# Slots of each expert place from one-hot products on the chip, in place of a slot table in device memory

## The chip, the cores and the metric

The kernel runs on one core of a Trainium2 chip. The metric is the device time of one execution in microseconds (us). Three runs of the kernel before took 1507.99 us in the median (1507.69 to 1508.86).

## The reference

One layer of a hybrid encoder over 512 tokens of width 1024: attention heads of three kinds, a layer norm, then a mixture of 32 experts, of which each token uses four, and a second layer norm. Only the routing and the experts matter here:

```python
def moe_ffn(x2d, router_w, router_b, w_gu, b_gu, w_dn, b_dn):
    logits = (x2d @ router_w + router_b).astype(jnp.float32)
    top_val, top_idx = lax.top_k(logits, TOP_K)          # TOP_K = 4 of 32
    gates = jax.nn.softmax(top_val, axis=-1)
    ...                                                  # rows sorted by expert
    def expert_block(args):
        xb, e = args
        hh = xb @ w_gu[e] + b_gu[e]
        glu = jnp.minimum(hh[:, 0::2], SWIGLU_LIMIT)
        lin = jnp.clip(hh[:, 1::2], -SWIGLU_LIMIT, SWIGLU_LIMIT)
        act = glu * jax.nn.sigmoid(SWIGLU_ALPHA * glu) * (lin + 1.0)
        return act @ w_dn[e] + b_dn[e]
    ...
    out = jnp.zeros((T, D), jnp.float32).at[row_tok].add(ys * row_gate[:, None])
```

An expert's weights are 8 MB for `w_gu` and 4 MB for `w_dn`, all in float32, so the 32 experts read some 400 MB from device memory.

## The kernel before

**Front part.** Projections, attention heads and the output projection (`w_o`) run for about 345 us. The 512 tokens are handled as four tiles of 128 (`tt` = 0 to 3). For each tile the residual row is normed (`normed`, ACT, DVE and POOL share it), written to `h_dram` by a POOL DMA, routed (`best_four`), given its position within each expert (`positions`) and its gate weights (`gates`).

**Places.** The experts are worked through in 32 places. Experts 0 and 1 have places 0 and 1, so their weights can be loaded before routing is known; the rest are ranked by how many tokens they have (`ranks`: `rank`, then `place`, a one-hot matrix from place to expert, and `eid`, the expert of each place). `TILES` says how many groups of 32 tokens a place has: three for most, two for the small ones (odd places 3 to 25, 30 and 31), four for place 12. Tokens beyond that go through a spare loop (`For_i`, L1220) whose count `ntrip` (computed in `rounds`) is read at run time; it has no trip in the profiled execution. At the entry of that loop SP waits on the semaphores of all DMA queues and the engines wait for one another.

**Slots.** A place must know for each of its slots the token to gather, the row of `y_dram` that its result is scattered to, and the gate. Before, this comes from a table in device memory. `table_rows` (DVE) works out the row of the table for each token and choice; `table_write` (POOL) writes four indirect DMAs per token tile, 16 in all. During place 0 `table_read` reads the table back with 13 DMAs issued by ACT into `TT`, in four variants of how slots lie on partitions, and `table_fit` adjusts them. `slots_of(e)` then picks one place's column out of `TT` with a multiplication, a sum and a cast on DVE. Place 1 alone, whose rows are needed early, gets its tokens from `slot_map` and `slots` (a float32 one-hot product).

**Loop over the places.** For place `e`, PE runs eight steps `k` of `gu_cols` (`hh`, L1088), then four of `dn_cols` of place `e-1` (`yy`, L1101). In between, in an order written out by hand for all engines (`manual_schedule`), stand the transposes of the activations (`thalf_cols`, L1147), the bias product (`bias_rows`, L1110) and the transposes of the next place's gathered rows (`transposed_rows`, L1074). These short products share two PSUM buffers `pt`; `hh` has one buffer only, so that place `e+1` cannot begin before DVE has read place `e`. `prepare(e+2)` at step `k` = 4 computes the slots of place `e+2` and gathers its rows; `store` scatters the results (L1166).

**Weights.** SP loads them in pieces of 1 MB, twelve per place, into a ring of 18 buffers (`raw`, `refill`, L896 and L898). Eighteen pieces are issued before place 0 starts; every further one waits until PE has finished with a buffer. From place 2 on the address comes from `eidI`.

Of the kernel before, what the change touches and what calls it, by code (L numbers as in the profile page):

```python
# [9 lines left out]
F32 = mybir.dt.float32  # L10
# [12 lines left out]
E, TOPK = 32, 4  # L23
# [14 lines left out]
def tile_encoder_layer(ctx: ExitStack, tc: tile.TileContext, a, out, dbg=None, stage=9):  # L38
# [622 lines left out]
    itok = lx.tile([P, 2, NT], F32, name="itok")  # L661
# [12 lines left out]
    posm = cst.tile([P, NT, E], F32, name="posm")  # L674
    R = cst.tile([P, NT, E, 3], F32, name="R")
# [60 lines left out]
    def positions(tt):  # L736

        dense = rt_w[tt][1]
        p = bank([P, E])
        for u in range(tt):  # L740
            nc.tensor.matmul(p, ones, sel[:, u, :], start=(u == 0), stop=False)
        nc.tensor.matmul(p, before, sel[:, tt, :], start=(tt == 0), stop=True)
        nc.vector.scalar_tensor_tensor(posm[:, tt, :], p, 1.0, dense, op0=OP.add, op1=OP.mult)
        nc.vector.tensor_scalar(posm[:, tt, :], posm[:, tt, :], -1.0, None, op0=OP.add)

    def gates(tt):
# [4 lines left out]
        over_k(R[:, tt, :, 2], eq[:, 1])  # L751
        nc.vector.tensor_mul(eq[:, 1], eq[:, 0], ik.unsqueeze(2).to_broadcast(b3))
        over_k(R[:, tt, :, 1], eq[:, 1])
        nc.vector.tensor_scalar(R[:, tt, :, 1], R[:, tt, :, 1], itok[:, 1, tt:tt + 1], None, op0=OP.add)
        nc.vector.tensor_copy(R[:, tt, :, 0], itok[:, 0, tt:tt + 1].to_broadcast([P, E]))

    def table_rows(tt):

        eq, _, g4, _ = rt_w[tt]
        nc.vector.tensor_copy(pay[:, tt, :, 2], g4)  # L760
        sx = lx.tile([P, E + TOPK], F32, name="sx", tag="sx", bufs=2)
        nc.vector.scalar_tensor_tensor(sx[:, 0:E], posm[:, tt, :], float(E), ie, op0=OP.mult, op1=OP.add)
        nc.vector.tensor_mul(eq[:, 1], eq[:, 0], sx[:, 0:E].unsqueeze(1).to_broadcast(b3))
        nc.vector.tensor_reduce(sx[:, E:E + TOPK], eq[:, 1], axis=AX.X, op=OP.add)
        nc.vector.tensor_copy(tix[:, tt, :], sx[:, E:E + TOPK])

    def table_write(tt):
        for k in range(TOPK):
            nc.gpsimd.indirect_dma_start(
                out=table[:, :], out_offset=bass.IndirectOffsetOnAxis(ap=tix[:, tt, k:k + 1], axis=0),  # L770
                in_=pay[:, tt, k, :], in_offset=None, bounds_check=P * E - 1, oob_is_err=False)
# [7 lines left out]
    def ranks(p):  # L779

        key, rank, eid = (mb.tile([P, E], F32, name=n) for n in ("key", "rank", "eid"))
# [5 lines left out]
        nc.vector.tensor_reduce(rank, w, axis=AX.X, op=OP.add)  # L787
        place = mb.tile([P, E, E], BF16, name="place")
# [6 lines left out]
        return rank, eid, eidI, place  # L795
# [26 lines left out]
    def places(tt):  # L822
# [3 lines left out]
        nc.vector.tensor_tensor(o, islot, posm[:, tt, 0:1].to_broadcast([P, P]), op=OP.is_equal)  # L826
# [27 lines left out]

    rp = mb.tile([P, E], F32, name="rp")
# [12 lines left out]
    pay = mb.tile([P, NT, TOPK, 3], F32, name="pay")  # L868
    nc.gpsimd.iota(pay[:, :, :, 0], pattern=[[P, NT], [0, TOPK]], base=0, channel_multiplier=1,
                   allow_small_or_imprecise_dtypes=True)  # L870
    nc.gpsimd.iota(pay[:, :, :, 1], pattern=[[TOPK * P, NT], [1, TOPK]], base=0, channel_multiplier=TOPK,
                   allow_small_or_imprecise_dtypes=True)
    table = dram.tile([P * E, 3], F32, name="table")
    empty = lx.tile([P, E, 3], F32, name="empty")
    nc.gpsimd.memset(empty[:, :, 0:2], float(BIG))
    nc.gpsimd.memset(empty[:, :, 2:3], 0.0)
    nc.gpsimd.dma_start(raw_ap(table, 0, [[3 * E, P], [1, 3 * E]]), empty.rearrange("p e c -> p (e c)"))
    tix = mb.tile([P, NT, TOPK], I32, name="tix")
# [107 lines left out]
    table_rows(0)  # L986
    table_write(0)
    places(0)
    table_rows(1)
# [12 lines left out]
    table_write(1)  # L1002
# [6 lines left out]
    table_rows(2)  # L1009
# [3 lines left out]
    table_write(2)  # L1013
# [11 lines left out]
    table_rows(3)  # L1025
# [15 lines left out]
    rank, eid, eidI, place = ranks(p)  # L1041
# [128 lines left out]
    def store(p, s, n):  # L1170
        y = mz.tile([P, 2, 512], F32, name="y", tag="y", bufs=2)
        ix, g = s
        for t in range(1, n):
            b, o, c = t // 2, (0, 0, 0, 256)[t], (0, 512, 256, 256)[t]
            nc.scalar.activation(y[:, b, o:o + c], p[:, b, o:o + c], AF.Copy, scale=g[:, t, 2:3])  # L1175
            scatter(y[:, b, o:o + c], ix[:, t, 1:2], D // c)
# [7 lines left out]

    TT = mb.tile([P, 4, E, 3], F32, name="TT")

    def table_read():
        def rd(dst, v, slot0):  # L1190
            n = dst.stop - dst.start
            nc.scalar.dma_start(TT[dst, v].rearrange("p e c -> p (e c)"),
                                raw_ap(table, slot0 * 3 * E, [[3 * E, n], [1, 3 * E]]))

        rd(slice(0, P), 0, 0)
        for g in range(4):
            for v in range(1, 4):
                rd(slice(32 * g, 32 * g + 32), v, 32 * (g // 2 if v == 1 else v))

    def table_fit():  # L1200
        for v in range(1, 4):
            nc.vector.tensor_scalar(TT[:, v, :, 1], TT[:, v, :, 1], 2.0 if v == 1 else 4.0,
                                    half if v == 1 else quarter, op0=OP.mult, op1=OP.add)

    def slots_of(e):

        n = 4 if TILES[e] == 4 else 3 if TILES[e] == 3 else 2
# [12 lines left out]
    with tc.For_i(0, n, 1):  # L1220
# [79 lines left out]
        scatter(y, iy)  # L1300


    yl, sl, bias = [], {}, {}
    py, ph, glu, sg, lin, aT, xg = {}, {}, {}, {}, {}, {}, {}

    def prepare(e):
# [284 lines left out]
```

## Time and profile before

| | us |
|---|---|
| median of three timed runs | 1507.99 |
| the profiled execution, its own time | 1503.06 |
| its span in the trace | 1501.3 |
| PE busy in the span | 1363.9 (91%) |
| DVE busy | 480.4 (32%) |
| ACT busy | 299.5 (20%) |
| POOL busy | 144.1 (10%) |

The 16 DMA engines moved 469.66 MB, 313 GB/s over the span and around 400 GB/s in the last two thirds. PE's busy time counts pipelined products whose ends are modelled, so it doesn't say alone that PE is the limit. The trace's times count from the start of the span.

### The profile page before, as it was taken

The page shows a single profiled execution, that of the slowest core. Times are in us where ns is not written, and L with a number is a line of the kernel's source. Part 1 is how long each engine was busy: PE and PEld are TensorE (multiplying, and loading weights), DVE is VectorE, ACT ScalarE, POOL GpSimd, SP SyncE. Part 2 cuts the span into 40 slices and gives each one's busy share as a digit, 9 for nine tenths or more (in the row PEclk, how much of TensorE's full clock was granted, in tenths as well). Part 3 has the DMA queues.
Part 4 walks back from the last instruction along what each step waited for, and adds up shares of the span by engine and source line. Part 5 has one row for each costly group of instructions (what it writes and reads, how often), then busy time and mean ns, then how long its engine had stood idle before and what let it go on. Part 6 is the DMA issues. An engine that isn't in the chain of part 4 may idle for free. (4 is left out here: it accounts for less than half of the span.)

```text
span 1501.3 us, 27744 instructions
## 1 busy us (share of the span) xinstructions
PE 1363.9 (91%) x11708; PEld 622.4 (41%) x11708; DVE 480.4 (32%) x1137; ACT 299.5 (20%) x553; POOL 144.1 (10%) x174
## 2 busy tenths in 40 slices
PE   7999998993449989999999989999998989999995
PEld 6888786893113323332332323332232322333232
DVE  5697658674321111211121111211111121111138
ACT  4345557410011111111111111111111111111110
POOL 3000000022310010001000011010100000000013
PEclk9999998897679999999999999999999999999888
DMA  8462102537258999999999999999999999999991
GB/s 229 145 228 82 43 13 72 184 147 322 82 178 331 376 400 387 405 406 406 406 407 401 405 399 406 389 402 396 404 396 390 405 399 404 398 403 402 406 385 74
DMA packets 93684, 469.66 MB, mean 313 GB/s; under 512 B 11487, under 2 KB 12567, under 8 KB 59509
## 3 DMA queue, kind: packets, MB, share of 16 engines
q1 hardware_dynamic: 83604, 445.29, 75.5%
q0 software_dynamic: 7920, 18.44, 3.9%
q10 hardware_dynamic: 2032, 4.13, 0.8%
q8 instruction: 93, 1.52, 0.4%
q14 instruction: 35, 0.28, 0.0%
HBM read 449.68 MB, written 23.01 MB: 315 GB/s over the span
## 5 line engine op out<-in xcount | busy, mean ns | idle before, releaser
L1088 PE MATMUL hh<-wr,xT 128*32 128x512 f32 x5312 | 618.5, 606 | 42.0 <-DMA wr<-in_w_gate_up_dram 18.1
L1088 PEld LDWEIGHTS hh<-wr,xT 128*32 128x32 f32 x5312 | 160.6, 111 | 411.9 <-issue 353.9
L1101 PE MATMUL yy<-wr,aT 128*32 128x512 f32 (+1 forms) x3200 | 286.7, 512 | 3.5 <-DMA wr<-in_w_down_dram 3.0
L1101 PEld LDWEIGHTS yy<-wr,aT 128*32 128x32 f32 x3200 | 100.2, 110 | 172.4 <-issue 133.6
L1120 DVE TENSOR_TENSOR glu<-hh,bt 128x768 f32<-128x768 f32 (+2 forms) x32 | 27.2, 849 | 367.7 <-PE hh L1088 345.4
L1166 POOL DMA_INDIRECT y_dram<-y,sloti x49 | 49.0, 999 | 718.4 <-ACT y L1175 568.2
L1214 DVE CAST sloti<-slot 128x6 int32<-128x6 f32 (+2 forms) x32 | 5.3, 164 | 287.6 <-DMA y_dram<-y,sloti 287.4
L1150 ACT ACTIVATE aT<-pt 128x384 f32<-128x384 f32 (+2 forms) x64 | 28.5, 447 | 280.7 <-PE pt L1147 261.4
L1175 ACT ACTIVATE y<-yy,slot 128x512 f32<-128x512 f32 (+1 forms) x49 | 27.5, 602 | 224.7 <-PE yy L1101 224.7
L1213 DVE TENSOR_REDUCE slot<-tw 128x9 f32<-128x288 f32 (+2 forms) x32 | 13.2, 413 | 163.5 <-ACT y L1175 163.3
L1075 ACT ACTIVATE xT<-pt 128x384 f32<-128x384 f32 (+2 forms) x62 | 27.6, 445 | 144.2 <-PE pt L1074 144.2
L1112 ACT ACTIVATE bt<-pt 128x512 f32<-128x512 f32 x32 | 19.1, 597 | 181.5 <-PE pt L1110 181.5
L201 PE MATMUL mm<-xh,wh 128*128 128x512 f32 x128 | 51.0, 399 | 0.6 <-DVE Qr L300 0.6
L203 PE MATMUL mm<-xh,wl 128*128 128x512 f32 x128 | 50.0, 391 | 0.0
L202 PE MATMUL mm<-xl,wh 128*128 128x512 f32 x128 | 49.9, 390 | 0.0
L1074 PEld LDWEIGHTS pt<-ident,xg 96*128 96x128 f32 (+2 forms) x248 | 21.8, 141 | 65.3 <-issue 51.2
L1079 POOL DMA_INDIRECT xg<-h_dram,sloti x30 | 29.8, 992 | 194.9 <-issue 120.6
L1110 PE MATMUL pt<-ball,oneh 128*128 128x512 f32 x64 | 38.4, 684 | 9.1 <-DVE oneh L1108 9.1
L131 DVE TENSOR_TENSOR wl<-raw,wh 128x1024 fp32r<-128x1024 f32 x32 | 39.0, 1221 | 20.5 <-ACT wh L130 20.5
L1074 PE MATMUL pt<-ident,xg 96*128 96x96 f32 (+2 forms) x248 | 32.1, 252 | 13.8 <-ACT bt L1112 13.8
L130 ACT ACTIVATE wh<-raw 128x1024 fp32r<-128x1024 f32 x32 | 33.6, 1054 | 32.5 <-PE mm L202 14.2
L1147 PEld LDWEIGHTS pt<-ident,glu 128*128 128x128 f32 x166 | 17.0, 140 | 53.2 <-issue 53.2
(369 smaller groups left out, 1564.6 us busy)
## 6 DMA issues: line engine op xcount, KB each, us to landing
wr<-in_w_gate_up_dram SPq DMA_DIRECT2D x256, 1024.0 KB
wr<-in_w_down_dram SPq DMA_DIRECT2D x128, 1024.0 KB
raw<-in_wp_dram SPq DMA_DIRECT2D x32, 512.0 KB
y_dram<-zero SPq DMA_DIRECT2D x16, 512.0 KB
wr<-y_dram SPq DMA_DIRECT2D x8, 1024.0 KB
xr<-in_xT_dram SPq DMA_DIRECT2D x2, 1024.0 KB
wr<-in_wp_dram SPq DMA_DIRECT2D x2, 1024.0 KB
hs<-in_x_dram ACTq DMA_DIRECT2D x2, 1024.0 KB
```

The source lines that it names most:

```text
L130: nc.scalar.activation(wh, r, AF.Copy)
L131: nc.vector.tensor_sub(wl, r, wh.bitcast(F32))
L201: nc.tensor.matmul(p[:, :n], wh[:, c, s], xh[:, k, :], start=(k == 0), stop=False)
L202: nc.tensor.matmul(p[:, :n], wh[:, c, s], xl[:, k, :], start=False, stop=False)
L203: nc.tensor.matmul(p[:, :n], wl[:, c, s], xh[:, k, :], start=False, stop=(k == KD - 1))
L1074: nc.tensor.transpose(p[:, k, 0:n], src[0:n, (4 * u + k) * P:(4 * u + k + 1) * P], ident[0:n, 0:n])
L1079: nc.gpsimd.indirect_dma_start(out=xg[0:n], out_offset=None, in_=h_dram[:, :], in_offset=bass.IndirectOffsetOnAxis(ap=it[0:n, :1], axis=0) ...
L1088: nc.tensor.matmul(p[32 * g:32 * g + 32, t, :], xT[:, k, 32 * t:32 * t + 32], w[:, 512 * g:512 * g + 512], start=(k == 0), stop=(k == KD - 1))
L1101: nc.tensor.matmul(p[32 * g:32 * g + 32, t // 2, o:o + c], aT[:, f, 32 * t:32 * t + 32], w[:, u * D + c * b:u * D + c * b + c], start=(f = ...
L1110: nc.tensor.matmul(p, o, ball, start=True, stop=True)
L1150: nc.scalar.activation(d, pv, AF.Copy)
L1166: nc.gpsimd.indirect_dma_start(out=raw_ap(y_dram, 0, [[D // n, T * TOPK * n], [1, D // n]]), out_offset=bass.IndirectOffsetOnAxis(ap=iy, a ...
```

## The change

The table, its writes and its reads are gone. `A` holds, per token tile, position, choice and gate of all experts side by side (in place of `posm` and `R`). For each place, `place_map` (DVE) picks the place's column out of `A`, makes a bfloat16 one-hot matrix of positions and six bfloat16 columns (token in tile, start of the tile, choice, and the gate split in three); `slots_of` multiplies them on PE (four products 128x6) and finishes slot, row and gate on DVE; `slots_spread` copies them to the other layouts by products with constant float32 matrices (one per further group of tokens). `prepare` has three parts, at `k` = 2, 4 and 6. The second half of `ranks` (`place`, `eid`, `eidI`) becomes `places_of` and moves from before the spare loop into step `k` = 1 of place 0, behind place 1's slots.

```diff
     def gates(tt):
...
-        over_k(R[:, tt, :, 2], eq[:, 1])
+        over_k(A[:, tt, 2], eq[:, 1])
...
-        over_k(R[:, tt, :, 1], eq[:, 1])
-        nc.vector.tensor_scalar(R[:, tt, :, 1], R[:, tt, :, 1], itok[:, 1, tt:tt + 1], None, op0=OP.add)
-        nc.vector.tensor_copy(R[:, tt, :, 0], itok[:, 0, tt:tt + 1].to_broadcast([P, E]))
-
-    def table_rows(tt):
...
-    def table_write(tt):
-        for k in range(TOPK):
-            nc.gpsimd.indirect_dma_start(
...
+        over_k(A[:, tt, 1], eq[:, 1])
...
+        return rank
+
+    def places_of(rank):
+
+        eid, b2 = mb.tile([P, E], F32, name="eid"), [P, E, E]
...
     places(0)
-    table_rows(1)
     best_four(2)
...
-    table_write(1)
     resid(3, 1)
...
     normed(3)
-    table_write(2)
     rows_of_first(1, 0)
...
+    def place_map(e):
+
+        if e < 2:
+            r = A[:, :, :, e]
+        else:
+            w = mz.tile([P, NT, 3, E], F32, name="tw", tag="tw", bufs=1)
+            r = mz.tile([P, NT, 3], F32, name="pr", tag="pr", bufs=2)
+            nc.vector.tensor_mul(w, A, place[:, e, :].unsqueeze(1).unsqueeze(1).to_broadcast([P, NT, 3, E]))
+            nc.vector.tensor_reduce(r, w, axis=AX.X, op=OP.add)
+        oh = mz.tile([P, NT, P], BF16, name="ohb", tag="ohb", bufs=1)
+        b3 = [P, NT, P]
+        nc.vector.tensor_tensor(oh, islot.unsqueeze(1).to_broadcast(b3), r[:, :, 0].unsqueeze(2).to_broadcast(b3),
+                                op=OP.is_equal)
+        rb = rbs[e % 2]
...
+        return oh, rb
+
+    def slots_of(e, oh, rb):
+
+        p = mp.tile([P, 512], F32, name="pt", tag="pt", bufs=2)
+        for tt in range(NT):
+            nc.tensor.matmul(p[:, 0:6], oh[:, tt, :], rb[:, tt, :], start=(tt == 0), stop=(tt == NT - 1))
...
+        return ix, r
+
+    def slots_spread(e, ix, r):
+        n = TILES[e]
+        p = mp.tile([P, 512], F32, name="pt", tag="pt", bufs=2)[:, 0:12].rearrange("p (v c) -> p v c", v=4)
+        for v in range(1, n):
+            nc.tensor.matmul(p[:, v, :], spread[v - 1], r[:, 0, :], start=True, stop=True)
+        nc.vector.tensor_copy(r[:, 1:n, :], p[:, 1:n, :])
...
+    def prepare(e, part):
+        if e < E and part == 0:
+            maps[e] = place_map(e)
+        if e < E and part == 1:
+            sl[e] = slots_of(e, *maps.pop(e))
+            if e > 0:
+                xg[e] = gather(sl[e][0][:, 0:1], e, 32 * TILES[e])
+        if e < E and part == 2:
+            slots_spread(e, *sl[e])
...
             if e == 0:
-                if k == 0:
-                    oh1 = slot_map(posm[:, :, 1])
+                if k in (0, 1):
+                    prepare(1, k)
                 if k == 1:
-                    xg[1] = gather(slots(oh1, lambda tt: R[:, tt, 1, :])[0], 1, 32 * TILES[1])
-                    table_write(3)
-                    table_read()
-                if k == 7:
-                    table_fit()
-                    for i in range(3):
-                        prepare(i)
+                    eid, eidI, place = places_of(rank)
+                if k in (2, 3):
+                    prepare(0, k - 2)
+                if k in (4, 5, 6):
+                    prepare(2, k - 4)
+                    if k < 6:
+                        prepare(k - 4, 2)
...
-            if k == 4 and e > 0:
-                prepare(e + 2)
+            if k in (2, 4, 6) and e > 0:
+                prepare(e + 2, k // 2 - 1)
```

POOL's queue from the norm of token tile 2 to the spare loop, before (`hs` are the rows being normed, `table` is the slot table):

```order
L700 TENSOR_TENSOR hs<-hs,gb 128x512
L701 TENSOR_TENSOR hs<-hs,gb 128x512
L706 DMA h_dram<-hs 128x1024
L769 DMA table<-pay,tix 4096x3 x8
L700 TENSOR_TENSOR hs<-hs,gb 128x512
L701 TENSOR_TENSOR hs<-hs,gb 128x512
L706 DMA h_dram<-hs 128x1024
L769 DMA table<-pay,tix 4096x3 x4
L1033 MEMSET xg_3698 128x1024
```

and now:

```order
L700 TENSOR_TENSOR hs<-hs,gb 128x512
L701 TENSOR_TENSOR hs<-hs,gb 128x512
L706 DMA h_dram<-hs 128x1024
L700 TENSOR_TENSOR hs<-hs,gb 128x512
L701 TENSOR_TENSOR hs<-hs,gb 128x512
L706 DMA h_dram<-hs 128x1024
L1022 MEMSET xg_3638 128x1024
```

Eight indirect DMAs stood ahead of the norm of the last token tile, and four behind it; the queue now goes straight from one norm to the next.

ACT's queue at place 0, behind the spare loop (`TT` is the table read back, `bt` the bias, `xT` the transposed rows of place 1), as a difference:

```order
-L1192 DMA TT<-table 128x96
-L1192 DMA TT<-table 32x96 x12
-L1112 ACT_TABLE_LOAD
-L1112 ACTIVATE bt<-pt 128x512
-L1075 ACTIVATE xT<-pt 128x384 x2
```

The thirteen reads of the table stood ahead of the copy of place 0's bias; the copy is now the first row there (under L1101).

PE's queue at place 0, now (`ohb` is the one-hot matrix, `rb` the six columns; before, four products of L1060 stood behind the first 24 of `hh` and nothing until the bias):

```order
L1077 MATMUL hh<-wr,xT 32x512 x24
L1200 MATMUL pt<-rb_2831,ohb 128x6
L1200 MATMUL pt<-rb_2831,ohb 128x6
L1200 MATMUL pt<-rb_2831,ohb 128x6
L1200 MATMUL pt<-rb_2831,ohb 128x6
L1077 MATMUL hh<-wr,xT 32x512 x24
L1200 MATMUL pt<-rb_2830,ohb 128x6
...
L1077 MATMUL hh<-wr,xT 32x512 x12
L1214 MATMUL pt<-slot,spread_2810 128x3
L1214 MATMUL pt<-slot,spread_2811 128x3
L1077 MATMUL hh<-wr,xT 32x512 x12
```

Every place has gained one group of four such products and one of one to three products with `spread`; place 0 carries those of places 0, 1 and 2.

## Rows read from the trace of the kernel before

**Rows 1.** Chain of waits in order of time: start us, length us, what.

```profile
886.85 7.00 PE yy L1101 x64
...
954.88 21.39 DMA wr<-in_w_gate_up_dram
```

**Rows 2.** SP's waits, 447 to 600 us: total us, times, longest us.

```profile
SPq L896 <- PE hh L1088: 49.4, 16, 16.4
```

**Rows 3.** SP's waits, 700 to 1380 us.

```profile
SPq L898 <- DMA wr<-in_w_gate_up_dram: 170.8, 80, 4.1
```

**Rows 4.** PE's waits for weights, whole span.

```profile
PEld hh L1088 <- DMA wr<-in_w_gate_up_dram: 40.8, 43, 3.3
...
PEld yy L1101 <- DMA wr<-in_w_down_dram: 13.1, 22, 1.5
```

**Rows 5.** Windows: length, busy of PE, PEld, DVE, ACT, POOL; PEclk, DMA share, GB/s.

```profile
344.00:371.00 27.00, 7.50 (x69) 7.00 (x67) 10.26 (x50) 1.12 (x4) 4.69 (x5) 0.74 1.01 417
371.00:405.00 34.00, 8.48 (x40) 3.31 (x44) 11.62 (x21) 0.87 (x2) 11.79 (x11) 0.51 0.06 20
...
425.00:447.00 22.00, 1.06 (x6) 0.61 (x4) 6.28 (x16) 4.88 (x6) 1.97 (x2) 0.58 0.34 108
447.00:460.00 13.00, 12.90 (x95) 3.93 (x99) 3.41 (x7) 0.49 (x1) 0.97 (x1) 0.79 0.55 201
```

**Rows 6.** Timeline, 345 to 400 us: start, busy, engine, line, operation; idle before it.

```profile
349.08 0.80 ACT L699 ACTIVATE hs<-hs,lnt 128x512 f32<-128x512 f32 x1
...
349.67 0.25 PE L776 MATMUL gen<-sel,ones 128*128 128x32 bf16 x4
...
377.70 1.28 POOL L700 TENSOR_TENSOR hs<-hs,gb 128x512 f32<-128x512 f32 x1
...
380.38 2.08 PE L832 MATMUL x<-o,hs 128*128 128x128 f32 x8 [26.14 <-POOL hs L701]
380.62 0.64 POOL L706 DMA_DIRECT2D h_dram<-hs  x1 [0.30 <-POOL hs L701]
...
383.76 1.23 DVE L786 TENSOR_TENSOR sg<-key 128x1024 f32<-128x1024 f32 x1 [28.40 <-DMA h_dram<-hs]
...
386.27 1.23 DVE L789 TENSOR_TENSOR place<-rank,rp 128x1024 bf16<-128x1024 f32 x1
...
390.05 2.59 DVE L794 CAST eidI<-eid 1x32 int32<-1x32 f32 x1
...
395.10 0.13 DVE L815 CAST ntrip<-xt 1x1 int32<-1x1 f32 x1
...
398.59 8.32 PE L1088 MATMUL hh<-wr,xT 128*32 128x512 f32 x48 [16.14 <-issue]
```

**Rows 7.** DMA issues of POOL: count, size, median us to landing.

```profile
h_dram<-hs POOLq DMA_DIRECT2D x4, 512.0 KB, 3.0
...
xg<-h_dram,sloti POOLq DMA_INDIRECT x30, 8.0
```

**Rows 8.** SP's waits, 340 to 470 us: the entry of the spare loop.

```profile
SPq L1220 <- DMA table<-pay,tix: 1.1, 1, 1.1
```

**Rows 9.** Timeline, 406 to 448 us: place 0 and the start of place 1.

```profile
406.84 1.05 PE L1060 MATMUL pt<-R,oh 128*128 128x3 f32 x8
...
424.61 0.55 PE L1074 MATMUL pt<-ident,xg 96*128 96x96 f32 x4
...
430.98 6.04 ACTq L1192 DMA_DIRECT2D TT<-table  x13
437.06 1.28 ACT L1112 ACT_TABLE_LOAD   x1 [52.44 <-DMA TT<-table]
...
444.40 0.96 DVE L1120 TENSOR_TENSOR glu<-hh,bt 128x768 f32<-128x768 f32 x1
...
447.10 10.53 PE L1088 MATMUL hh<-wr,xT 128*32 128x512 f32 x72 [7.20 <-ACT sg L1135]
```

**Rows 10.** Timeline of PE, 610 to 628 us, a place in the middle.

```profile
610.32 7.91 PE L1088 MATMUL hh<-wr,xT 128*32 128x512 f32 x72
...
626.90 1.12 PE L1110 MATMUL pt<-ball,oneh 128*128 128x512 f32 x2
627.95 2.78 PE L1088 MATMUL hh<-wr,xT 128*32 128x512 f32 x24
```

More of the change, by code (lines that the diff above doesn't have):

```diff
@@ L779, in ranks @@
     def ranks(p):
-        key, rank, eid = (mb.tile([P, E], F32, name=n) for n in ("key", "rank", "eid"))
+        key, rank = (mb.tile([P, E], F32, name=n) for n in ("key", "rank"))
         b2 = [P, E, E]
@@ L794, in ranks @@
         nc.vector.tensor_copy(eidI, eid[0:1, :])
-        return rank, eid, eidI, place
+        return eid, eidI, place
     def rounds(p, rank):
@@ L853, in tile_encoder_layer @@
         nc.gpsimd.memset(quarter[s, :], float(i))
+    spread = [mb.tile([P, P], F32, name="spread%d" % i) for i in range(3)]
+    for i, t in enumerate(spread):
+        w = x4("w", [P, P], I32)
+        if i == 0:
+            nc.gpsimd.iota(w.rearrange("p (t b s) -> p t b s", t=2, b=2), pattern=[[32, 2], [0, 2], [1, 32]], base=0,
+                           channel_multiplier=-1)
+        else:
+            nc.gpsimd.iota(w.rearrange("p (b s) -> p b s", b=4), pattern=[[0, 4], [1, 32]], base=32 + 32 * i,
+                           channel_multiplier=-1)
+        nc.gpsimd.tensor_scalar(t, w, 0.0, None, op0=OP.is_equal)
     rp = mb.tile([P, E], F32, name="rp")
@@ L866, in tile_encoder_layer @@
             r, i = r + j - i, j
[L868 to L878, printed above, removed]
+    rbs = [mb.tile([P, NT, 6], BF16, name="rb%d" % i) for i in range(2)]
+    for t in rbs:
+        nc.gpsimd.iota(t[:, :, 0], pattern=[[0, NT]], base=0, channel_multiplier=1,
+                       allow_small_or_imprecise_dtypes=True)
+        nc.gpsimd.iota(t[:, :, 1], pattern=[[P, NT]], base=-BIG, channel_multiplier=0,
+                       allow_small_or_imprecise_dtypes=True)
     def raw_mr():
@@ L1040, in tile_encoder_layer @@
         nc.scalar.activation(xT[0][:, 4 * u:4 * u + 4, 0:32 * TILES[0]], x0[u][:, :, 0:32 * TILES[0]], AF.Copy)
-    rank, eid, eidI, place = ranks(p)
+    rank = ranks(p)
     cum, cend, s1, s2, short, ntrip = rounds(p, rank)
@@ L1183, in keep @@
         return h, l
[L1187 to L1207, printed above, removed]
-        w = mz.tile([P, 4, 3, E], F32, name="tw", tag="tw", bufs=1)[:, 0:n]
-        r = mz.tile([P, 4, 3], F32, name="slot", tag="slotr", bufs=4)
-        ix = mz.tile([P, 4, 2], I32, name="sloti", tag="sloti", bufs=4)
-        nc.vector.tensor_mul(w, TT[:, 0:n].rearrange("p v e c -> p v c e"),
-                             place[:, e, :].unsqueeze(1).unsqueeze(1).to_broadcast([P, n, 3, E]))
-        nc.vector.tensor_reduce(r[:, 0:n], w, axis=AX.X, op=OP.add)
-        nc.vector.tensor_copy(ix[:, 0:n], r[:, 0:n, 0:2])
-        return ix, r
+    def place_map(e):
+        if e < 2:
+            r = A[:, :, :, e]
+        else:
+            w = mz.tile([P, NT, 3, E], F32, name="tw", tag="tw", bufs=1)
[7 more added lines that the diff above has]
+        rb = rbs[e % 2]
+        t = mz.tile([P, NT], F32, name="prt", tag="prt", bufs=2)
+        nc.vector.tensor_copy(rb[:, :, 2], r[:, :, 1])
+        nc.vector.tensor_copy(rb[:, :, 3], r[:, :, 2])
+        nc.vector.tensor_sub(t, r[:, :, 2], rb[:, :, 3])
+        nc.vector.tensor_copy(rb[:, :, 4], t)
+        nc.vector.tensor_sub(rb[:, :, 5], t, rb[:, :, 4])
+        return oh, rb
@@ new lines, in slots_spread @@
+    def slots_spread(e, ix, r):
[4 more added lines that the diff above has]
+        nc.vector.tensor_copy(r[:, 1:n, :], p[:, 1:n, :])
+        nc.vector.tensor_scalar(ix[:, 1:2], r[:, 1, 1:2], 2.0, half, op0=OP.mult, op1=OP.add)
+        if n > 2:
+            nc.vector.tensor_scalar(ix[:, 2:n], r[:, 2:n, 1], 4.0, quarter, op0=OP.mult, op1=OP.add)
@@ L1300, in tile_encoder_layer @@
         scatter(y, iy)
-    yl, sl, bias = [], {}, {}
+    yl, sl, bias, maps = [], {}, {}, {}
     py, ph, glu, sg, lin, aT, xg = {}, {}, {}, {}, {}, {}, {}
-    def prepare(e):
-        if e < E:
-            sl[e] = slots_of(e)
-            if e > 1:
-                xg[e] = gather(sl[e][0][:, 0, 0:1], e, 32 * TILES[e])
+    def prepare(e, part):
[7 more added lines that the diff above has]
+            slots_spread(e, *sl[e])
     def finish(e, part):
@@ L1341, in last_rows @@
             for tt in range(NT):
-                nc.tensor.matmul(p[0:E, tt, :], R[:, tt, :, 2], ident, start=True, stop=True)
+                nc.tensor.matmul(p[0:E, tt, :], A[:, tt, 2], ident, start=True, stop=True)
             nc.scalar.activation(gt[0], p[0:E], AF.Copy)
```

44 lines of the change are left out of this document (17 added, 27 removed).

## The prediction

> **What bounds the kernel now.** I read the chain of waits first. It ends in the experts' weights: from 955 us on, long stretches of it are weight loads, ahead of that it alternates with PE's products [rows 1]. So there are two limits, and the next question is which holds where. SP's own waits tell it. Between 447 and 600 us SP waits for PE to give a buffer back, 16.4 us of it in one piece [rows 2]: all 18 buffers are full and PE sets the pace. From 700 us on it waits for its own earlier loads [rows 3]: the loads set the pace, and PE is short of weights for 40.8 + 13.1 = 53.9 us in all [rows 4]. A stream of loads that never stops can end earlier only if it gets going earlier, so I looked for holes in it. The windows show them [rows 5]: DMA is full up to 371 us, nearly empty (0.06) for 34 us, and again at 0.34 for the 22 us from 425 and at 0.55 for the 13 us from 447. The hole is 34 x 0.94 + 22 x 0.66 + 13 x 0.45 = 52 us. More than that can't be won ahead of the steady part.
>
> The timeline tells what makes each hole. First hole: ACT is done with the last token tile at 349.88 us, but POOL takes it up only at 377.70, since eight table writes stand before it in its queue. PE waits 26.14 us for POOL, the rows reach memory with a DMA issued at 380.62, DVE's ranking waits 28.40 us for it, and place 0 starts at 398.59 [rows 6]. Second hole: ACT must issue 13 reads of the table before the bias of place 0; it waits 52.44 us, the reads go out from 430.98 on, and place 1 starts on PE at 447.10, although place 0's last product but four transposes ended at 425.16 [rows 9].
>
> **The change, part by part.**
>
> *Start of place 0.* Without the table, POOL takes up tile 3 when ACT is done: 349.9 + 3.6 us (377.70 to the end of the DMA's issue at 381.26) = 353.5 [rows 6]. How long that DMA takes beside full weight loads isn't shown; 3.0 us is the median of its kind, 8.0 that of the gathers under load [rows 7], so the rows land between 356.5 and 361.5; I take the later, since DMA is full there [rows 5]. DVE then ranks: 383.76 to 386.27 stays, the part from there to 392.64 moves into place 0, the rest to 395.23 stays [rows 6], together 2.5 + 2.6 = 5.1 us, so the trip count is there at 366.6. From that to PE's first product passed 398.59 - 395.23 = 3.4 us: 370. But something else now comes later. At the entry of the spare loop SP waited 1.1 us for a table write that nothing there reads [rows 8]; so it waits for every DMA, and the eighteen pieces of weights land at 371 us [rows 5], plus 0.5 MB of rows now among them (1.3 us at 417 GB/s), 372.3. With 2.5 us to release the engines (by the 3.4 above, less the wait), place 0 starts at **375**, 23.6 us earlier. Bounds: 366 if the loop doesn't wait for the weights, 380 if the rows take twice the longer time.
>
> *Place 0 itself* took 425.16 - 398.59 = 26.6 us, and half a pair of transposes, 0.5 us. PE loses four products of L1060, 1.05 us [rows 9], and gains three groups of four bfloat16 products and three of two float32 ones. A group of four bfloat16 products of 32 columns took 0.25 us [rows 6]; two float32 ones are half of L1060's, 0.53. That is 3 x 0.78 - 1.05 = 1.3 us. DVE becomes a cover that may be too short: behind place 1's slots it now does the moved part of the ranking, three operations like the 1.23 us one [rows 6], and then place 0's map, so it is ready some 15 us after the start, where PE arrives after 14; the bias behind two more groups costs a similar wait. I take 2.5 us for both, bounds 0 and 8. SP's first load for place 2 needs `eidI`, which comes some 4 us later than its buffer; DMA has nothing else to load then. Sum: 31 us.
>
> *Start of place 1.* No table read stands before the bias, so DVE can read place 0's sums when PE is done. What stays is the single buffer `hh`: two reads and a clamp took 444.40 to 447.0, 2.6 us [rows 9], some of it beside the transposes; I take 2. Place 1 starts at 375 + 31 + 2 = **408** in place of 447.1, 39.1 us earlier. PE then comes without a long pause: in the 22 us before 447 its clock was mostly the lower one, 1.2 of 2.4 GHz (0.58 in the mean) [rows 5], and the first three steps took 10.53 us, against 7.91 later [rows 9, 10]. That gives 2.6 us more: 41.7.
>
> *All later places* meet the same loads, the same ring of buffers, full as before, and the same products, so the shift lasts to the end except for what PE has to do in addition: 0.25 + 0.53 us for a place of three groups, 0.5 for one of two. Where PE is the limit, up to about 600 us, this is places 1 to 4: 4 x 0.75 = 3 us; behind that the loads set the pace, and 26 x 0.7 = 18 us disappear in the 53.9 us for which PE is short of weights. If that cover were gone, they would all be paid. DVE's longer maps stand where it waits for PE or for scatters anyway; POOL's new constants are made some 70 us before it is next needed. The last part, from the final weights on, is untouched.
>
> The sum: 41.7 - 3.0 = 38.7 us. The profiled execution took 1503.06 us around a span of 1501.3; it would become 1464.4. The median of the timed runs lies 4.9 us above it, so the prediction is 1507.99 - 38.7 = **1469 us**.
>
> *A rule that speaks against it.* The bias product stands between column-split products too, and its two passes of 512 columns take 1.05 us from its start to that of the next `hh` product [rows 10], so I give the new groups no extra for their place. The Trainium skill (TensorEngine Tiling, Key Properties) says that a change of tiling mode drains TensorE; each new group is a 128x128 block between 128x32 ones, so by it every place pays two more drains each way. The rows show no gap of its size at the bias; what it would cost if paid in full is the last rival.
>
> **Rivals.**
>
> *The loop doesn't wait for the weights.* Then place 0 starts at 366 to 368, and the gain is 45 to 48 us: 1461. For it: only one short wait shows that SP drains there. Against: nothing else explains a wait for a table write at that line.
>
> *Place 0 gets a wait of its own.* DVE carries 4 us of ranking plus three maps within 30 us, all in the order of its queue, and PE waits at each group. If that costs 8 us more than I took, the lower clock comes back as well: gain 38.7 - 8 - 2.6 = 28, 1480.
>
> *PE becomes the limit over all places,* and it ends slower. The mechanism is the two new groups in each place: PE stops at each until the products ahead have left, and at the second also for DVE, which is held by the scatters. It decides from (41.7 + 53.9) / 30 = 3.2 us per place on, the shift and the cover used up. Each stop at the price of a whole bias block, 1.05 us, before and after both groups makes 4.2 us per place and 30 x 4.2 - 95.6 = 30 us: 1538. Against: the bias block streams two passes of 512 columns, the new ones 24 and 12 columns in all.
>
> *It does nothing,* since the loads are the limit: speaks against it that DMA was empty in front of the steady part [rows 5].
>
> **How the numbers follow.** My forecast, 1469, has 0.65, the loop that doesn't wait 0.18, the wait in place 0 0.10, PE as the limit 0.05, no effect 0.02. The most that the hole allows is 52 us, 1456; above, 28 us less some 6 for waits not foreseen gives 1486. What lies outside is about 0.12, mostly the last two. Within 0.2%, some 3 us, a measurement can't tell this kernel from no change. Faster: 0.93, same 0.02, slower 0.05.
>
> **What would show it.** Right: POOL's norm of tile 3 at 350 us, no L832 wait on PE; place 0's first product near 375 with SP waiting for weights at the loop; place 1 near 408; DMA without the two holes; the tail 39 us earlier. Wrong: SP or PE waiting for DVE at place 0 by more than a few us, PE's waits for weights gone in the middle (then the new groups cost more than 0.8), or a start of place 0 that some other DMA holds.

## Result and profile after

The changed kernel took 1464.31 us in the median of four runs (1460.20 to 1467.05), the kernel before 1507.84 beside it on the same chip (1504.57 to 1508.86): a ratio of 0.9713, 95% interval 0.9685 to 0.9740. The forecast was 1469 in a range of 1456 to 1486. The profiled execution took 1464.26 us around a span of 1462.5, 38.8 us less than the span before; the sum had said 38.7.

| us | before | after |
|---|---|---|
| span of the profiled execution | 1501.3 | 1462.5 |
| PE busy | 1363.9 | 1372.7 (94%) |
| DVE busy | 480.4 | 550.7 (38%) |
| POOL busy | 144.1 | 130.5 (9%) |
| mean rate of the DMA engines | 313 GB/s | 321 GB/s |

The timeline of the kernel after, 348 to 410 us, is the counterpart of [rows 6] and [rows 9]; columns are start, length, engine, line, operation, and in brackets the idle time before and what ended it:

```profile
349.53 1.40 POOL L700 TENSOR_TENSOR hs<-hs,gb 128x512 f32<-128x512 f32 x1 [9.43 <-PE gen L758]
...
352.89 0.57 POOL L706 DMA_DIRECT2D h_dram<-hs  x1 [0.30 <-POOL hs L701]
361.50 1.23 DVE L768 TENSOR_TENSOR sg<-key 128x1024 f32<-128x1024 f32 x1 [4.38 <-DMA h_dram<-hs]
366.64 0.13 DVE L803 CAST ntrip<-xt 1x1 int32<-1x1 f32 x1
376.00 0.69 DVE L1185 TENSOR_TENSOR ohb<-islot,A 128x512 bf16<-128x512 f32 x1 [9.22 <-DMA wr<-in_w_down_dram]
376.14 8.10 PE L1077 MATMUL hh<-wr,xT 128*32 128x512 f32 x48 [19.50 <-DMA wr<-in_w_down_dram]
...
388.81 0.17 DVE L782 CAST eidI<-eid 1x32 int32<-1x32 f32 x1
...
390.40 0.24 PE L1200 MATMUL pt<-rb,ohb 128*128 128x6 bf16 x4 [0.69 <-DVE rb L1193]
...
398.27 1.10 PE L1099 MATMUL pt<-ball,oneh 128*128 128x512 f32 x2 [1.04 <-DVE oneh L1097]
...
408.04 9.63 PE L1077 MATMUL hh<-wr,xT 128*32 128x512 f32 x72 [1.90 <-DVE lin L1109]
```

POOL takes up tile 3 at 349.53 in place of 377.70, and PE has no wait for it any more. DVE has the rows at 361.50, the trip count at 366.64. Then nothing computes for 9.2 us: DVE's next operation and PE's first product of place 0 both come behind a load of weights. Place 0 starts at 376.14 and place 1 at 408.04, where it was 398.59 and 447.10.

SP's waits, 340 to 420 us (total us, times, longest us), tell what those 9.2 us are; before, one short wait stood there [rows 8]:

```profile
SPq L1222 <- DVE ntrip L803: 12.5, 1, 12.5
...
SPq L1223 <- DMA wr<-in_w_down_dram: 5.3, 2, 2.9
SPq L887 <- DVE eidI L782: 4.3, 1, 4.3
...
SPq L1223 <- DMA wr<-in_w_gate_up_dram: 1.4, 1, 1.4
SPq L1223 <- DMA h_dram<-hs: 0.8, 1, 0.8
```

L1223 is the entry of the spare loop. SP waits there for loads of weights that nothing in the loop reads.

Windows of the kernel after (length, busy of PE, PEld, DVE, ACT, POOL; PEclk, DMA share, GB/s), beside [rows 5]:

```profile
371.00:380.00 9.00, 3.86 (x20) 0.99 (x24) 1.36 (x6) 1.28 (x1) 0.00 (x0) 0.50 0.30 112
380.00:405.00 25.00, 23.27 (x202) 7.40 (x194) 10.79 (x43) 0.60 (x1) 2.88 (x2) 0.97 0.81 290
405.00:425.00 20.00, 18.11 (x150) 6.29 (x150) 7.91 (x20) 3.98 (x6) 0.00 (x0) 0.91 0.78 292
425.00:447.00 22.00, 22.00 (x228) 7.83 (x224) 7.67 (x17) 3.48 (x6) 1.85 (x2) 1.00 0.97 350
447.00:460.00 13.00, 13.00 (x122) 3.99 (x118) 0.47 (x5) 0.98 (x2) 1.15 (x2) 1.00 0.97 388
```

Of the hole of 34 us at a DMA share of 0.06, some 9 us at 0.30 are left, and the share stays near 0.8 until place 1 is under way (0.81, 0.78). The second hole (0.34 and 0.55) is gone. Summed as in the prediction, 16.5 us of empty time are left from 371 to 460 us, where it had 52.

**Does the lead last?** One mark per stage shows it: the bias product, one group per place on PE (places 1, 18 and 30), and SP's first issue of a place's last four weight pieces (places 2, 7 and 30). PE and SP in the timeline of the kernel before:

```profile
466.52 1.13 PE L1110 MATMUL pt<-ball,oneh 128*128 128x512 f32 x2
996.39 1.12 PE L1110 MATMUL pt<-ball,oneh 128*128 128x512 f32 x2
1390.71 1.12 PE L1110 MATMUL pt<-ball,oneh 128*128 128x512 f32 x2
...
457.69 9.33 SPq L898 DMA_DIRECT2D wr<-in_w_down_dram  x4
646.45 8.92 SPq L898 DMA_DIRECT2D wr<-in_w_down_dram  x4
1410.67 8.50 SPq L898 DMA_DIRECT2D wr<-in_w_down_dram  x4
```

The same marks of the kernel after:

```profile
426.88 1.12 PE L1099 MATMUL pt<-ball,oneh 128*128 128x512 f32 x2
969.73 1.12 PE L1099 MATMUL pt<-ball,oneh 128*128 128x512 f32 x2
1352.31 1.13 PE L1099 MATMUL pt<-ball,oneh 128*128 128x512 f32 x2
...
417.72 6.76 SPq L894 DMA_DIRECT2D wr<-in_w_down_dram  x3
612.20 7.08 SPq L894 DMA_DIRECT2D wr<-in_w_down_dram  x4
1369.95 8.46 SPq L894 DMA_DIRECT2D wr<-in_w_down_dram  x4
```

PE leads by 39.6 us at place 1, by only 26.7 at place 18, and by 38.4 at place 30. The loads lead by 40.0, then 34.2, then 40.7. The loads' lead is 40.0 us again at place 12 (issued at 812.23 us before, at 772.23 now), while that of PE falls on to place 18. So PE does lose time with the added products, 13 us in 17 places; but while it still has buffers full of weights, that is a loss of stock, not of time. Once the stock is gone, both kernels end with the loads, whose lead is whole again.

### The profile page after: what moved, and what is told of

Read it like the earlier page. It is cut to its first block, busy times and chain, and to the rows that moved or that the text cites. A ratio compares the mean times of both kernels' runs of the same rounds, so it can differ in the third digit from the quotient of the medians.

```text
span 1462.5 us, 28498 instructions
## 1 busy us (share of the span) xinstructions
PE 1372.7 (94%) x11930; PEld 633.6 (43%) x11930; DVE 550.7 (38%) x1499; ACT 299.7 (20%) x553; POOL 130.5 (9%) x163
## 5 line engine op out<-in xcount | busy, mean ns | idle before, releaser
L1077 PEld LDWEIGHTS hh<-wr,xT 128*32 128x32 f32 x5312 | 157.6, 110 | 369.6 <-issue 340.3
L1203 DVE TENSOR_REDUCE slot<-pt 128x1 f32<-128x2 f32 x32 | 5.1, 160 | 454.7 <-PE pt L1200 454.7
L1215 DVE COPY slot<-pt 128x6 f32<-128x6 f32 (+2 forms) x32 | 5.3, 164 | 157.4 <-PE pt L1214 157.4
L1101 ACT ACTIVATE bt<-pt 128x512 f32<-128x512 f32 x32 | 19.1, 597 | 205.4 <-PE pt L1099 205.4
L130 ACT ACTIVATE wh<-raw 128x1024 fp32r<-128x1024 f32 x32 | 33.6, 1053 | 31.6 <-PE mm L202 14.2
L931 PE MATMUL mm<-wh,cTh 128*128 128x256 f32 x128 | 36.5, 285 | 0.4 <-DVE catm L551 0.4
L213 PE MATMUL mm<-wh,xh 128*128 128x256 f32 x128 | 36.8, 288 | 0.0
```

Source lines behind the costliest of these rows:

```text
L130: nc.scalar.activation(wh, r, AF.Copy)
L213: nc.tensor.matmul(p[:, i, :], xh[:, k, s], wh[:, c, :], start=(k == 0), stop=False)
L931: nc.tensor.matmul(p[:, i, :], cTh[:, k, s], wh[:, c, :], start=(j == 0), stop=False)
L1077: nc.tensor.matmul(p[32 * g:32 * g + 32, t, :], xT[:, k, 32 * t:32 * t + 32], w[:, 512 * g:512 * g + 512], start=(k == 0), stop=(k == KD - 1))
```

## Experiments

Since the places from 1 on behave alike in nearly all runs, each profiled execution is cut into four by three rows: DVE's first operation of the ranking (the rows of tile 3 have landed), PE's first product of place 0, and that of place 1.

| us | ratio of timed medians, 95% interval | rows landed | to place 0 | to place 1 | to the end |
|---|---|---|---|---|---|
| before | 1 | 383.8 | 14.8 | 48.5 | 1054.2 |
| the change | 0.9713 (0.9685 to 0.9740) | 361.5 | 14.6 | 31.9 | 1054.5 |
| the change, again | 0.9721 (0.9700 to 0.9742) | 364.2 | 14.6 | 31.4 | 1053.0 |
| before, table writes behind tile 3 | 0.9995 (0.9978 to 1.0013) | 363.0 | 36.8 | 48.4 | 1054.1 |
| before, table read at place 1 | 0.9906 (0.9881 to 0.9932) | 383.1 | 14.9 | 28.4 | 1059.4 |
| no spare loop | 0.9657 (0.9636 to 0.9678) | 366.7 | 4.1 | 31.7 | 1056.3 |
| 3 pieces behind the loop | 0.9695 (0.9669 to 0.9721) | 362.8 | 8.4 | 31.4 | 1053.6 |
| the same, again | 0.9685 (0.9665 to 0.9705) | 367.8 | 8.5 | 31.9 | 1053.6 |
| 6 pieces behind the loop | 0.9679 (0.9657 to 0.9700) | 365.7 | 8.4 | 31.7 | 1054.3 |
| 3 pieces behind, bias first | 0.9668 (0.9645 to 0.9692) | 363.0 | 8.4 | 31.6 | 1053.1 |
| bias first | 0.9711 (0.9686 to 0.9735) | 364.0 | 14.7 | 31.6 | 1053.3 |
| places ranked ahead of the loop | 0.9706 (0.9685 to 0.9727) | 364.0 | 13.3 | 31.0 | 1051.3 |
| new products twice | 0.9733 (0.9706 to 0.9761) | 360.8 | 13.9 | 32.9 | 1054.0 |
| new products four times | 0.9947 (0.9926 to 0.9969) | 359.6 | 14.8 | 38.0 | 1079.9 |

The column of the rows varies by 8 us among kernels whose program is the same up to there but for the number of weight pieces issued (359.6 to 367.8 behind the change). The scatter stands already at POOL's norm of token tile 0, which starts between 311.50 and 319.71 us in these kernels, well ahead of the steps that are read here. It is in every time below, and a single profiled execution can't tell 5 us; the two columns behind it can, and the last one can tell 3 us or so (1051.3 to 1056.3 among kernels that do the same work there).

**1. The table's writes, moved behind tile 3.** In the kernel before:

```diff
     table_rows(0)
-    table_write(0)
...
-    table_write(1)
     resid(3, 1)
...
     normed(3)
-    table_write(2)
+    for tt in range(3):
+        table_write(tt)
```

> The kernel before, with all twelve early table writes behind the norm of token tile 3 in POOL's queue. Theory (the loop's entry waits for every DMA): the norm starts at 350 us and PE no longer waits for POOL, but the twelve writes then run one after the other from 353 us on (three at 6.8 us each beside the weights, nine at 2.9 us, 4.7 us to land), and the loop waits for them: place 0 starts at 400 to 404 us instead of 398.6, time 1505 to 1515 us. Rival (only the order in POOL's queue matters): place 0 starts at 376 to 382 us, time 1487 us.

Measured: 1504.48 us, ratio 0.9995, just under the 1505 that was expected, and far from the rival's 1487. PE's wait for POOL at tile 3 went, the rows landed 20.8 us earlier, and all of it was lost again before place 0. SP's wait at the loop (340 to 420 us):

```profile
SPq L1219 <- DMA table<-pay,tix: 24.8, 1, 24.8
```

PE's first product of place 0 there:

```profile
399.83 7.83 PE L1087 MATMUL hh<-wr,xT 128*32 128x512 f32 x48 [40.53 <-issue]
```

The trip count was ready at 372.15, and place 0 waited for the last of twelve table writes, issued at 395.06. Nothing in the loop reads the table: its entry waits for DMAs that its body has no use for. So the writes cost some 22 us (36.8 against the 14.6 of the change) wherever they stand ahead of the loop; the change gains them because it has no writes, not because tile 3 goes first.

**2. The table read at place 1.** In the kernel before, `table_read` moved from place 0 to `k` = 0 of place 1, `table_fit` and the first three `prepare` to `k` = 4 of place 1:

```diff
                     table_write(3)
-                    table_read()
-                if k == 7:
-                    table_fit()
-                    for i in range(3):
-                        prepare(i)
             elif k == 0:
                 finish(e - 2, 0)
+                if e == 1:
+                    table_read()
...
+            if k == 4 and e == 1:
+                table_fit()
+                for i in range(3):
+                    prepare(i)
```

> The kernel before, with the reads of the table at the start of place 1 and their fitting and the slots of places 0 to 2 at its step 4. Theory (the second hole is the bias of place 0 and DVE's reading of its sums standing behind the table): place 1 starts at 428 us instead of 447, then loses some 5 us at its steps 5 and 6 for the late slots; time 1488 to 1496 us. Rival (place 1 starts when the loads or other work allow): place 1 at 445 us or later, time 1506 to 1512 us.

Measured: 1489.74 us, as expected. Place 1 starts 28.4 us after place 0, not 48.5, so the thirteen reads ahead of ACT's bias copy were the second hole. Some of it comes back inside place 1, where PE waits for DVE's queue with its three maps (PE's timeline):

```profile
426.34 9.63 PE L1088 MATMUL hh<-wr,xT 128*32 128x512 f32 x72 [1.89 <-DVE lin L1120]
...
448.88 2.04 PE L1110 MATMUL pt<-ball,oneh 128*128 128x512 f32 x2 [3.96 <-DVE oneh L1108]
```

By the table the gain of the change in this pair of executions divides like this (their norms of tile 0 start 0.7 us apart, so little of it is scatter): rows 22.3 us earlier (383.8 to 361.5), places 0 and 1 closer by 16.6 us (48.5 to 31.9), together 38.9 and, with 0.2 us of the column between, the 39.1 us by which place 1 starts earlier.

**3. No spare loop.** In the changed kernel; it leaves out the loop for tokens beyond the places, which has no trip here.

```diff
-    n = nc.values_load(ntrip, min_val=0, max_val=40)
-    with tc.For_i(0, n, 1):
...
```

> The changed kernel without the spare loop, which has no trip with these inputs: left out are the reading of the trip count, the loop's entry and its body. Theory (the loop's entry, waiting for all weight pieces, sets the start of place 0): PE starts place 0 as soon as ACT has copied its rows, at 363 us instead of 376.1, time 1451 us. Rival (the rows or the weights of place 0 set it): start not before 372 us, time 1460 to 1464 us.

Measured: 1453.12 us, ratio 0.9657. Place 0 came at 370.76, not near 363: 5.2 us of that are rows that landed later in this run, the rest is an underestimate, since place 0 still waits for DVE, 4.1 us after the rows (the trace names L796, in the count of the trips; which of its results PE needs there isn't shown). Against the change it starts 10.5 us earlier after the rows, and that is the price of the loop's entry with all that it waits for.

**4. Three pieces of weights issued behind the loop** instead of ahead of it, in the changed kernel:

```diff
-    for _ in range(MO):
+    for _ in range(MO - 3):
         refill()
...
     order.__enter__()
+    for _ in range(3):
+        refill()
```

> The changed kernel with three of the eighteen weight pieces issued behind the loop instead of ahead of it. Theory (the wait for the pieces sets the start): the wait ends at 364 us, ahead of the trip count (366.8), place 0 starts at 370 instead of 376.1 us, and PE sets the pace there, so all of it is kept: 1458 us. Rival (loads are what counts, and three pieces are put off by 8 us): place 0 at 370 us, but no gain or up to 3 us lost in the time, 1464 to 1467 us.

Measured: 1457.84 us, as expected; place 0 starts 8.4 us after the rows, not 14.6, SP has no wait for weights at the loop any more, and all behind it is unchanged. The gain is read from these columns: the interval of the ratio (0.9669 to 0.9721) still overlaps that of the change. Run again beside its variants:

> The kernel with three of the eighteen pieces behind the loop once more, beside its variants. Theory (the loop waits for the outstanding loads): as in the first run, ratio to the kernel before 0.967 to 0.972, place 0 some 17 us after DVE has the rows of the last tile.

Measured: 1459.07 us, ratio 0.9685. (Where this expectation and those of experiments 5 and 9 say "after the rows", their 17.2, 12.8 and 23.3 us were counted from the last tile's output projection, L820, some 9 us ahead of the rows; the table counts from the rows.)

**5. Six pieces behind the loop**, the same edit with 6.

> Six pieces behind the loop instead of three. Theory: with three behind, place 0 started 17.2 us after DVE had the rows; without the loop, 12.8 us. The trip count itself is there about 5 us after the rows, so with six behind the loads end before it, and place 0 starts 13 to 17 us after the rows: 0 to 4 us earlier than with three, 1454 to 1458 us. Rival: the empty time of DMA is what counts, not the start of place 0; DMA then stands still for 7.5 us more before the loop (three pieces at 2.5 us), and the kernel ends up to 7.5 us later than with three behind, about 1465 us.

Measured: 1458.91 us, ratio 0.9679, place 0 again 8.4 us after the rows. DVE's trip count and PE's first product in this run:

```profile
370.83 0.13 DVE L803 CAST ntrip<-xt 1x1 int32<-1x1 f32 x1
...
374.14 7.89 PE L1077 MATMUL hh<-wr,xT 128*32 128x512 f32 x48 [11.04 <-issue]
```

The 3.3 us from the one to the other are what the loop's entry takes by itself (3.5 before [rows 6]). Three pieces are enough; from there on the trip count holds place 0. The rival fell too: in the 9 us ahead of place 0 the DMA share was 0.02, with three behind 0.56 and 0.55 in its two runs, and yet the part from place 1 on took 1054.3 us, as in the others. Some 5 us more of idle DMA ahead of place 0 cost nothing that can be told here. That the time at which PE begins to give buffers back is what counts fits this and the runs above.

**6. The new products twice and four times**, to price them and find where their cover ends:

```diff
-        for tt in range(NT):
+        for tt in [*range(NT)] * 2:
             nc.tensor.matmul(p[:, 0:6], oh[:, tt, :], rb[:, tt, :], start=(tt == 0), stop=(tt == NT - 1))
...
-        for v in range(1, n):
+        for v in [*range(1, n)] * 2:
             nc.tensor.matmul(p[:, v, :], spread[v - 1], r[:, 0, :], start=True, stop=True)
```

> The changed kernel with every slot product on PE done twice (the same values written again). One place then costs PE 0.4 to 0.7 us more. Theory (PE sets the pace only in the first places, the loads behind): 2 to 5 us slower than the changed kernel, 1466 to 1469 us. Rival (PE sets the pace over all places): 30 x 0.58 = 17 us slower, 1481 us.

> The changed kernel with every slot product on PE done four times; a place costs PE 1.3 to 2.2 us more. Theory (the cover is what PE is short of weights, some 40 us): it is used up and PE becomes the limit: 27 to 39 us slower than the changed kernel, 1491 to 1503 us. Rival (the loads keep the pace whatever PE has in addition): at most the first places' 9 us, 1473 us.

Measured: 1465.19 and 1497.85 us, beside 1463.89 of the changed kernel on the same chip. Twice is a little under what its theory gave and within the uncertainty of once, so PE doesn't set the pace over all places; four times is not hidden and lies in its theory's range. Groups by line (busy us, mean ns) of the changed kernel:

```profile
L1214 PE MATMUL pt<-slot,spread 128*128 128x3 f32 x102 | 16.5, 258 | 0.0
...
L1200 PE MATMUL pt<-rb,ohb 128*128 128x6 bf16 x128 | 8.1, 168 | 0.7 <-DVE rb L1193 0.7
```

and with four times the products, with PEld's waits for weights under them:

```profile
L1214 PE MATMUL pt<-slot,spread 128*128 128x3 f32 x408 | 51.0, 254 | 0.0
...
L1200 PE MATMUL pt<-rb,ohb 128*128 128x6 bf16 x512 | 17.7, 166 | 0.7 <-DVE rb L1193 0.7
```

```profile
PEld hh L1077 <- DMA wr<-in_w_down_dram: 2.6, 5, 1.5
...
PEld hh L1077 <- DMA wr<-in_w_gate_up_dram: 0.8, 1, 0.8
```

The triple addition is 34.5 + 9.6 = 44.1 us of PE. Of it 6.6 are paid in place 0 (38.0 for 31.4), and 26.9 from place 1 on (1079.9 for 1053.0); the other 10.6 disappeared, and with them PE's waits for weights. A single addition, 14.7 us, costs 1.5 in place 0 and 1.0 behind it; 12.2 disappeared. So some 11 us of cover were left behind the change, as exactly as the last column tells.

**7. The bias product first.** The trace of the change has PE waits of 5 us for DVE at the bias product of two places, the first at place 3 (PE's timeline):

```profile
497.22 2.04 PE L1099 MATMUL pt<-ball,oneh 128*128 128x512 f32 x2 [5.04 <-DVE oneh L1097]
```

DVE's queue had the slots ahead of it. From place 1 on this run puts the bias ahead of them:

```diff
-            if k in (2, 4, 6) and e > 0:
+            if k in (2, 5, 7) and e > 0:
                 prepare(e + 2, k // 2 - 1)
-            if k == 5:
+            if k == (4 if e > 0 else 5):
                 bias[e] = bias_rows(e)
```

> The changed kernel with the bias product at step 4, the slot products at step 5 and the spreading at step 7. PE waited 5.0 us twice for DVE's one-hot matrix of the bias, which stands behind a cast that waits for scatters. Theory: both waits go, the one at place 3 while PE sets the pace, so 2 to 7 us are won: 1457 to 1462 us. Rival (the wait only moves to the spreading): PE waits as long at step 7, 1464 us.

Measured: 1463.57 us, the same as 1463.89. Neither outcome that I had put down: the waits did not move to the spread, they went, and still nothing was gained. The bias of place 3 and, from PEld's waits, the shortage of weights in this run:

```profile
492.36 1.12 PE L1099 MATMUL pt<-ball,oneh 128*128 128x512 f32 x2
```

```profile
PEld hh L1077 <- DMA wr<-in_w_gate_up_dram: 30.1, 42, 3.3
```

against 19.1 us of the same wait in the change. PE is earlier in the middle (the bias product of place 18 at 954.55 us, against 971.85 when the change ran again; some 3 us of that are the product's new place) and waits for weights later.

**8. Three behind the loop and bias first, together.**

> Three pieces behind the loop, and in each place the bias product at step 4, the slots at step 5 and the spread at step 7. By what the bias-first run alone showed (PE's two 5.0 us waits for DVE went, but shortage of weights took their place), the same time as with three behind alone, within 0.3%. Rival: with the earlier start PE is ahead of the loads for longer and the 5 us at place 3 come back: 1453 us.

Measured: 1456.34 us, ratio 0.9668; beside three behind alone (0.9685) it can't be told from no difference, as expected, and the rival's gain at place 3 doesn't show (1053.1 us from place 1 on, 1053.6 with three behind alone). Among the kernels that keep the loop it has the lowest ratio. Against the change measured again the intervals part (it ends at 0.9692, that of the change begins at 0.9700), against the change measured first they overlap by a little (0.9685). So it is some 0.5% faster than the change, and by the columns that is the start of place 0; against three or six behind alone no gain is shown.

**9. The places ranked ahead of the loop**, as before the change:

```diff
     cum, cend, s1, s2, short, ntrip = rounds(p, rank)
+    eid, eidI, place = places_of(rank)
...
-                if k == 1:
-                    eid, eidI, place = places_of(rank)
```

> The changed kernel with the second half of the ranking (place, eid, eidI) back ahead of the loop, as before the change. Theory: SP's waits for the loads at the loop end at about the same time whether DVE needs 5 us or 12 us for its part (the trip count came 9.2 us ahead of place 0), so place 0 starts within 1 us of the changed kernel's place in time after the rows (23.3 us), its waits for DVE of 0.7 and 1.0 us go, SP no longer waits 4.3 us for eidI; place 1 starts 0 to 2 us earlier, time 1462 to 1465. Rival: the trip count is what holds place 0, and it starts 7 us later: 1471.

Measured: 1461.86 us, ratio 0.9706. The loads still end the wait at the loop (place 0 13.3 us after the rows), PE's wait of 0.69 us and SP's for `eidI` are gone, the one of 1.04 us for the bias stayed. Within the uncertainty of the change: moving this part into place 0 bought nothing as long as the loads hold the loop.

## Why the prediction was right

**The limits and the holes.** The reading that a stream of loads can end earlier only by getting going earlier held: the loads lead by 40.0 us at place 2 and by 40.7 at the end. What I made of the hole's 52 us as the most that can be won isn't borne out: six pieces behind the loop made the hole ahead of place 0 longer and lost nothing. The start of place 0 counts, not the share of DMA ahead of it.

**Start of place 0**, 375 predicted, 376.1 measured, and by its own steps: end of POOL's issue 353.5 predicted and 353.46 measured, rows 361.5 and 361.50, trip count 366.6 and 366.64. That the clock times agree to a tenth is luck: when the change ran again, the rows came at 364.2, the trip count at 369.4 and place 0 at 378.9. What was right were the lengths between them. From the end of POOL's issue to the rows passed 8.04 us, where I took 8.0 since DMA is full there (8.0 to 9.2 in all runs that issue it beside the loads, 2.5 in the kernel before), and from the rows to place 0 14.6, where I had 13.5. Two terms in that missed and cancelled: the loads were not done at 372.3 (the DMA share is still 0.82 from 371 to 374 us), and behind them less than the 2.5 us that I took was left to release the engines. That the entry of the loop would then wait for the weights, read from one wait of 1.1 us [rows 8], is shown by experiments 1, 3 and 4. The first rival, that it doesn't wait, would have needed a start at 366 to 368.

**Place 0 and place 1.** 31 us for place 0 and 2 for the buffer `hh`, 33, where it took 31.9. DVE's waits were 0.69 + 1.04 = 1.7 us for the 2.5 I took; SP waited 4.3 us for `eidI`, predicted 4. Place 1 at 408, measured 408.04. The rival with a wait of 8 us more in place 0 did not come.

**The clock, a term that was mis-sized.** I took the first three steps of place 1 from 10.53 to 7.91 us, 2.6 us. They took 9.63, so 0.9. Place 0 ends with a pause for the sums, and from 405 to 425 us the granted clock was 0.91 in the mean. In the run with the new products doubled, and in that with the places ranked ahead of the loop, the same steps took 7.93; why the clock was full there, and not in the others, isn't settled.

**The added products, mis-sized in two ways that cancel.** Their price was right. From the bias product of place 8 to that of place 10, a stretch in which PE never stops, it went like this (PE's timeline before, then after):

```profile
685.34 1.13 PE L1110 MATMUL pt<-ball,oneh 128*128 128x512 f32 x2
743.77 1.13 PE L1110 MATMUL pt<-ball,oneh 128*128 128x512 f32 x2
```

```profile
651.96 1.12 PE L1099 MATMUL pt<-ball,oneh 128*128 128x512 f32 x2
711.80 1.12 PE L1099 MATMUL pt<-ball,oneh 128*128 128x512 f32 x2
```

That is 58.43 and 59.84 us: 1.41 more for one place of three groups and one of two, where I had 0.78 + 0.5 = 1.28. Over 17 places the lead of PE falls by 13.0 us, 0.76 each with all that is in it. I let places 1 to 4 pay 3 us for good, since PE sets the pace there. The loads' lead did fall, by 5.7 us until 612 us, but it was back at place 12; no run shows by what. From place 1 to the end the change takes 1054.5 us, before 1054.2: a loss of 0.3, and I had 3.0 - 2.6 = 0.4 for it. As far as that column tells, the terms were each too large by about as much.

**The cover was smaller than I read it.** I took the 53.9 us of PEld's waits [rows 4] for the cover; two smaller rows of the same view (4.1 and 1.5 us) I left out. The change's products, some 0.7 x 30 = 21 us, and the 11 us left behind it by experiment 6 make about 32. Weight loads into PE overlap its products, so a wait of PEld is not always one of PE: for the rows of 40.8 us and 13.1 us of PEld, PE itself waited 18.1 and 3.0 us. These 21.1 us are too little for the cover, so no one row gives it; in the change PE's own waits for weights behind place 0 are 6.3 + 2.9 + 1.8 = 11.0 us, which is what experiment 6 found left. The last rival would have decided from (39 + 32) / 30 = 2.4 us per place, not from 3.2; four times the products, about 0.7 + 44.1 / 32 = 2.1 us per place, came near to it at 0.9947.

**The drain.** In the middle of the run the group of four stands between two steps like this (PE's timeline after):

```profile
904.27 2.78 PE L1077 MATMUL hh<-wr,xT 128*32 128x512 f32 x24
906.99 0.25 PE L1200 MATMUL pt<-rb,ohb 128*128 128x6 bf16 x4
907.17 2.78 PE L1077 MATMUL hh<-wr,xT 128*32 128x512 f32 x24
```

From the start of the step ahead to the group 2.72 us pass, where steps that follow one another start some 2.57 us apart (7.91 us for three, 2.78 for one [rows 10]); from the group to the next `hh` product 0.18 us, and no idle time stands ahead of either. So the group takes some 0.33 us of PE with all that belongs to it; the 1.05 us each way of the last rival is not there. The Trainium skill (TensorEngine Tiling (Array Packing), Key Properties) says that a change of tiling mode drains TensorE. If it does here, at this place both changes together fit into those 0.33 us.

**Profile and median.** The sum, 38.7 us, met the profiled pair, 38.8. The timed medians moved by 43.5, because the profiled execution before lay 4.9 us below its median, and that of after on its own. I carried the 4.9 over; with a scatter of 8 us in the front part alone I count it as chance (the kernel before, run again beside the experiments, took 1502.27 to 1509.51 us), and it is the whole difference between 1469 and 1464.3.

## To carry to other kernels

An instruction that waits for DMAs whose data it doesn't need, as the entry of this loop with a count read at run time does, makes the transfers ahead of it urgent, whoever reads it: look at what is outstanding there before shortening the way to it, and issue prefetches behind it that are not needed first. Where a pool of filled buffers stands between loads and compute, the loss of one engine in the middle is a loss of stock; only the lead of the stream that ends last is worth time, so compare two traces by the time of the same mark at the start, the middle and the end. Before counting a wait as cover for new work, find out on which engine it is time, by doubling the work until it shows.

## What was not expected of the hardware

The table's indirect writes took far longer beside the weights than alone. POOL's timeline in experiment 1, three writes beside the loads and two after them:

```profile
355.00 1.07 POOL L769 DMA_INDIRECT table<-pay,tix  x1 [0.31 <-issue]
363.88 1.24 POOL L769 DMA_INDIRECT table<-pay,tix  x1 [7.81 <-DMA table<-pay,tix]
370.04 0.97 POOL L769 DMA_INDIRECT table<-pay,tix  x1 [4.93 <-DMA table<-pay,tix]
...
392.67 0.98 POOL L769 DMA_INDIRECT table<-pay,tix  x1 [1.40 <-DMA table<-pay,tix]
395.06 0.98 POOL L769 DMA_INDIRECT table<-pay,tix  x1 [1.41 <-DMA table<-pay,tix]
```

One follows another after 8.9 and 6.2 us beside the loads (DMA share 0.99 from 344 to 371 us) and after 2.4 us without them (0.01 from 380 to 400 us), though each moves the same few bytes. Behind a wait of PE the next product can run at half speed: the bias of place 3 took 2.04 us after its wait of 5.04 (granted clock 0.66 from 492 to 502 us), and 1.12 without it in experiment 7 (1.00 from 487 to 497 us). The wait need not be long: with four times the products, place 0's bias took 1.90 us after a wait of 0.91 (granted clock 0.60 from 400 to 404 us), where in the change it took 1.10 after one of 1.04. What makes the front part differ by up to 8 us from run to run is not shown.
